# A hybrid two-layer block on one core: values and keys transposed on VectorE and through DRAM, and an output product in another order

## The chip, the cores and the metric

One core of one Trainium2 chip. The metric is the device time of one execution in microseconds (us), the median over runs. The engines named are TensorE (PE), VectorE (DVE), ScalarE (ACT), GpSimd (POOL) and SyncE (SP); each works through its own queue in order, and the chip's 16 DMA engines move data between DRAM and on-chip memory.

## The reference, cut to what matters

The whole program is two layers on 1024 tokens of width 1024, in float32. Layer 0 mixes tokens with retention (four heads) and with a gated delta rule (four heads of 128 by 128), layer 1 with a gated linear recurrence; each is followed by a feed-forward part with a short convolution. The change lies almost wholly in layer 0's delta rule and in the product that ends a mixer:

```python
q_d = l2norm(q_d.reshape(b, t, GDN_HEADS, GDN_DK))
k_d = l2norm(k_d.reshape(b, t, GDN_HEADS, GDN_DK))
...
lmat = jnp.where(strict, jnp.einsum('bhnid,bhnjd->bhnij', k_beta, kc) * decay, 0.0)
rhs = jnp.concatenate([vc * bc, k_beta * jnp.exp(gc)[..., None]], axis=-1)
sol = lax.linalg.triangular_solve(lmat + jnp.eye(c, dtype=jnp.float32), rhs,
                                  left_side=True, lower=True)
...
v_new = u_n - jnp.einsum('bhcd,bhdv->bhcv', w_n, s)
o = jnp.einsum('bhcd,bhdv->bhcv', qd_n, s) + jnp.einsum('bhij,bhjv->bhiv', a_n, v_new)
s = s * cd_n + jnp.einsum('bhcd,bhcv->bhdv', kt_n, v_new)
...
y = jnp.concatenate([y_r, y_d.reshape(b, t, GDN_WIDTH)], axis=-1).astype(hn.dtype)
return y @ w_out
```

The recurrence runs chunk by chunk. The kernel inverts the triangular matrix once per chunk instead of solving with it, and works on eight chunks of 128 tokens.

## The kernel before, in words

Activations lie transposed, channels on the 128 partitions and the 1024 tokens along the free axis, in two halves of 512. Every weight product is made of three matmuls of 128x512 in a reduced format (`mm3`, lines 313 to 315): high part of the weight by high and by low part of the input, low part of the weight by the high part. ACT makes the high part of a weight (L267) and DVE the low part (L268), some steps ahead, from loads that SP issues (L257). This stream of matmuls, "projection" below, fills PE; a counter, `slot`, advances with each group of three, and everything else is hung between the groups: `after(n, f)` runs f n groups later, and a lane (`gdn`, `ret`) is a queue of generators that is taken one step further every so many groups. So the program is written in an order, and a scheduler then sets each engine's queue from it, by which its order can differ from the text's.

The mixer of layer 0, in time: convolutions of keys; A matrices per head; a substitution by rows on 32x32 blocks (`subst`, L1338 its last step on DVE) whose result goes to DRAM (`t_dram`) and comes back by blocks (L1353); then four merges, one per head, that assemble the inverse: 32x32 products L1369, L1378 and L1382, and 64x64 products L1392 and L1398, with ACT's copies L1372, L1385/L1386, L1394 and L1399 between them. The lane's generators for the merges follow `subst`, which yields 11 times after its store. Meanwhile heads of q and v are projected and convolved (`conv_head`, L1264 to L1269), and stored to `q_dram` and `v_dram`.

The scan (`scans`, L1446 on) then goes through the eight chunks. `scan_load` fetches v and q of a chunk. `scan_inside` makes, from a mask (L1453) and exponentials on ACT (L1455, L1457), the scores within the chunk: L1461 transposes v on PE, four heads, and DVE multiplies by a column (L1462); L1465 is keys times q, L1466 its product with the mask; L1473 transposes the keys, and L1474 multiplies them. `scan_state` takes the state through: L1485 keys times state, L1491 the inverse times v, copied by ACT (L1493), L1498 the state's update, L1509 the output, and then `normalise`: squares and sums, a power on POOL (L1422), a multiplication and a transpose on DVE (L1424, L1426), and eight groups later four stores from ACT's queue (L1431). Beside the scan runs retention, with a rotation of its q and k by cosines and sines on DVE (L1538, L1540, L1541) and POOL (L1542).

After the scan the mixer's eight outputs are gated (L1775 for the four of retention), split into high and low parts (ACT L586, DVE L587) and multiplied by the output weights in `part`, four of the inputs at a time (u = 0, 1). For the first half of the tokens the first four outputs form a group with a PSUM bank each: all four take inputs 4, 5, 6, 0 (u = 0), and then each output in turn takes 7, 1, 2, 3 (u = 1). The recurrent mixer of layer 1 ends in the same function.

## Time and profile before

| | |
|---|---|
| median of 3 runs | 2148.48 us (2148.06 to 2148.73) |
| profiled execution, its own time | 2149.09 us |
| its span, first to last instruction | 2147.3 us |
| clock granted to PE | 0.999 |
| PE, DVE, ACT, POOL busy | 99%, 79%, 50%, 5% |
| instructions | 29614 |

The 1.8 us between span and time lie around the span. In the rows of the profile, an engine's group of instructions is given as line, engine, operation, tile written <- tiles read, count, total busy time, mean duration; "idle before" is the time for which the engine stood still ahead of them, and what ended it. Matmuls overlap in the array, so a matmul's duration is longer than the distance from one start to the next.

### The profile page before, as it was taken

How to read it: one execution, taken by the hardware profiler on the slowest of the kernel's cores; microseconds unless marked ns; L12 is line 12 of the kernel's file. 1: busy time of each engine (PE TensorE's matmuls, PEld its weight loads, DVE VectorE, ACT ScalarE, POOL GpSimd, SP SyncE). 2: the span in 40 equal slices, each digit the busy share in tenths (PEclk: the TensorE clock that was granted, in tenths of full speed). 3: DMA queues.
4: the chain of work that ended last, by engine and by line, in shares of the span. 5: the costliest groups of instructions: out<-in, count | busy, mean ns of one | idle time of the engine just before them, and what ended most of it. 6: DMA issues, size and time to landing. Idle time of an engine off the chain costs nothing.

```text
span 2147.3 us, 29614 instructions
## 1 busy us (share of the span) xinstructions
PE 2131.8 (99%) x10652; PEld 1776.5 (83%) x10652; DVE 1704.7 (79%) x2581; ACT 1074.1 (50%) x1732; POOL 96.8 (5%) x114
## 2 busy tenths in 40 slices
PE   9999999999999999999999999999999999999998
PEld 7877888887888888888888888888888888888887
DVE  7995677766999989888766786778999889888645
ACT  6444522234665555555324476755655555554221
POOL 0102022200000000000000000000000000000001
PEclk9999999999999999999999999999999999999999
DMA  5354433543145435438725312252354445375542
GB/s 187 93 168 126 136 94 88 173 146 114 50 163 178 152 141 191 157 113 275 240 99 198 89 50 82 68 157 64 123 181 167 146 154 176 118 267 183 176 169 84
DMA packets 237171, 307.98 MB, mean 143 GB/s; under 512 B 62912, under 2 KB 125920, under 8 KB 237024
## 3 DMA queue, kind: packets, MB, share of 16 engines
q1 hardware_dynamic: 201344, 299.60, 41.8%
q10 hardware_dynamic: 34656, 5.97, 1.5%
q8 instruction: 84, 1.38, 0.3%
q0 software_dynamic: 1024, 0.53, 0.1%
q14 instruction: 63, 0.52, 0.1%
HBM read 215.27 MB, written 90.74 MB: 143 GB/s over the span
## 4 chain that ended last, share of the span: by engine, by line
PE 64%; issue 30%; DVE 3%; DMA 2%; POOL 0%; ACT 0%; SPq 0%; POOLq 0%; DVEq 0%; ACTq 0%
PE ps L313 19%; PE ps L315 19%; PE ps L314 19%; PE pc L313 1%; PE pc L314 1%; PE pc L315 1%; DVE h L973 0%; DVE l L1332 0%; DVE l L1334 0%; PE pc L1491 0%; PE pc L1577 0%; PE pc L1465 0%; PE ps L1509 0%; PE ps L1607 0%; DVE h L1303 0%
## 5 line engine op out<-in xcount | busy, mean ns | idle before, releaser
L313 PE MATMUL ps<-s,whi 128*128 128x512 f32 (+1 forms) x2704 | 1053.6, 390 | 2.5 <-ACT s L586 1.4
L314 PE MATMUL ps<-s,whi 128*128 128x512 f32 (+1 forms) x2704 | 1048.2, 388 | 1.2 <-DVE s L587 0.7
L315 PE MATMUL ps<-s,wlo 128*128 128x512 f32 (+1 forms) x2704 | 1047.5, 388 | 0.0
L267 ACT CAST whi<-raw 128x512 fp32r<-128x512 f32 (+1 forms) x620 | 377.0, 613 | 634.5 <-PE ps L314 499.7
L313 PEld LDWEIGHTS ps<-s,whi 128*128 128x128 f32 x2704 | 507.8, 188 | 108.2 <-ACT s L586 2.3
L314 PEld LDWEIGHTS ps<-s,whi 128*128 128x128 f32 x2704 | 508.0, 188 | 104.5 <-DVE s L900 1.8
L315 PEld LDWEIGHTS ps<-s,wlo 128*128 128x128 f32 x2704 | 507.7, 188 | 104.4 <-DVE wlo L268 0.6
L268 DVE TENSOR_TENSOR wlo<-raw,whi 128x512 fp32r<-128x512 f32 (+1 forms) x620 | 418.0, 680 | 64.0 <-ACT whi L267 55.2
L828 DVE SCALAR_TENSOR_TENSOR t<-halo,cols,t 128x1024 f32<-128x1024 f32 x176 | 221.7, 1281 | 2.1 <-ACT t L826 1.0
L801 DVE TENSOR_TENSOR halo<-ps,kept 128x512 f32<-128x512 f32 (+1 forms) x138 | 92.0, 667 | 76.4 <-PE ps L315 75.6
L811 DVE TENSOR_TENSOR h<-ps,h 128x512 f32<-128x512 f32 x112 | 77.3, 690 | 79.1 <-PE ps L315 79.1
L826 ACT ACTIVATE t<-halo,cols 128x1024 f32<-128x1024 f32 x88 | 109.6, 1247 | 18.0 <-DVE halo L801 9.9
L796 ACT COPY kept<-ps 128x512 f32<-128x512 f32 (+1 forms) x138 | 77.0, 558 | 11.0 <-PE ps L315 9.5
L533 DVE TENSOR_TENSOR h<-ps,h 128x512 f32<-128x512 f32 (+1 forms) x72 | 45.2, 630 | 42.0 <-PE ps L315 41.8
L916 DVE TENSOR_TENSOR t<-t 128x1024 f32<-128x1024 f32 x44 | 53.7, 1221 | 0.0
L911 ACT ACTIVATE t<-t 128x1024 f32<-128x1024 f32 x44 | 46.8, 1063 | 10.0 <-DVE t L828 10.0
L852 ACT CAST t<-t 128x512 fp32r<-128x512 f32 x56 | 34.0, 622 | 34.7 <-DVE t L916 32.7
L401 ACT ACTIVATE t<-h 128x512 f32<-128x512 f32 (+1 forms) x49 | 27.3, 563 | 44.2 <-DVE h L533 44.2
L313 PE MATMUL ps<-s,s 128*128 128x256 f32 (+1 forms) x144 | 46.0, 320 | 0.0
L314 PE MATMUL ps<-s,s 128*128 128x256 f32 (+1 forms) x144 | 45.8, 318 | 0.0
L315 PE MATMUL ps<-s,s 128*128 128x256 f32 (+1 forms) x144 | 45.8, 318 | 0.0
L1266 DVE SCALAR_TENSOR_TENSOR t<-halo,cols,t 128x1024 f32<-128x1024 f32 x33 | 41.9, 1278 | 2.9 <-ACT t L1264 2.6
(337 smaller groups left out, 2113.3 us busy)
## 6 DMA issues: line engine op xcount, KB each, us to landing
raw<-in_ffn_up_dram SPq DMA_DIRECT2D x176, 256.0 KB, 2.7
s<-pf_dram SPq DMA_DIRECT2D x112, 256.0 KB, 5.1
sf_dram<-t SPq DMA_DIRECT2D x72, 256.0 KB, 2.5
raw<-in_ffn_w_dram SPq DMA_DIRECT2D x64, 256.0 KB, 3.0
t<-sf_dram SPq DMA_DIRECT2D x58, 256.0 KB, 4.2
pf_dram<-t SPq DMA_DIRECT2D x56, 256.0 KB, 2.6
pf_dram<-lo SPq DMA_DIRECT2D x56, 256.0 KB, 2.6
raw<-in_mix_in_dram SPq DMA_DIRECT2D x52, 256.0 KB, 3.0
```

What stands on the lines that cost most here:

```text
L267: self.nc.scalar.copy(hi[:, 0:w], raw[:, 0:w])
L268: eng.tensor_tensor(lo[:, 0:w], raw[:, 0:w], f32(hi[:, 0:w]), ALU.subtract)
L313: mm(ps, whi, xhi, start=start, stop=False)
L314: mm(ps, whi, xlo, start=False, stop=False)
L315: mm(ps, wlo, xhi, start=False, stop=stop)
L796: A.copy(kept[o], ps)
L801: V.tensor_tensor(dst(i, j), v(ps), v(kept[k]), ALU.add)
L811: V.tensor_tensor(h(*to[o]), ps.rearrange("p (h c) -> p h c", c=256), h(*to[o]), ALU.add)
L826: A.activation(t, buf[:, 2:2 + T], AF.Identity, scale=w(0), bias=self.col(f"ffn_cb{layer}", tile_i))
L828: V.scalar_tensor_tensor(t, buf[:, 2 + j:2 + j + T], w(j), t, ALU.mult, ALU.add)
L911: A.activation(tg, tg, AF.Silu)
L916: V.tensor_tensor(tg, tg, tv, ALU.mult)
```

## The change

Five things. (1) A convolved head of v is transposed on DVE in 32x32 blocks into the buffer that its convolution no longer needs, and four DMAs from SP's queue store it so that it lies transposed in `v_dram`, in runs of 32 numbers; `scan_load` then brings v as the scan wants it, and L1461's transposes go. (2) Keys are treated likewise: `turn_keys(0)` for heads 0 and 1 after the two gates, `turn_keys(1)` for 2 and 3 after v's first head; their four DMAs each are issued from ACT's queue six groups later, `scan_load` fetches them from a new `k_dram`, and L1473's transposes go. (3) In `normalise` the multiplication and transpose come two groups later, and the stores after nine groups instead of eight. (4) `subst` yields 12 times at its end instead of 11, so that the merges begin later. (5) In `part`, the second four inputs of a group of outputs are taken input by input, each over all the group's outputs, and the sums are added to the residual at the end.

```diff
--- before.py
+++ after.py
@@ -515,6 +515,20 @@
         for ms in groups:
             ps = {m: self.pp(both=True)[:, 0:w] for m in ms}
             for u in range(2):
+                if u == 1 and len(ms) > 1:
+                    hold = self.qpos
+                    ws = [self.quarter((name + "b", m), 0, hold) for m in ms]
+                    for kt in range(len(ys) - 4):
+                        c = slice(kt * P, (kt + 1) * P)
+                        yh, yl = (a[:, c0:c0 + w] for a in ys[4 + kt][n])
+                        for m, (hi, lo) in zip(ms, ws):
+                            self.mm3(ps[m], hi[:, c], lo[:, c], yh, yl, False, kt == len(ys) - 5)
+                            self.slot()
+                    for m in ms:
+                        h = self.H[m][:, sl]
+                        self.nc.vector.tensor_tensor(h, ps[m], h, ALU.add)
+                        each(m, h)
+                    continue
                 for m in ms:
                     if kept is None:
                         hi, lo = self.quarter((name + "ab"[u], m))
@@ -1145,6 +1159,7 @@
         tc = self.tc
         self.q_dram = tc.dram_tile([NCH, P, HALF], F32, name="q_dram")
         self.ry_dram = tc.dram_tile([4, NCH, P, P], F32, name="ry_dram")
+        self.k_dram = tc.dram_tile([NCH, P, HALF], F32, name="k_dram")
         self.v_dram = tc.dram_tile([NCH, P, HALF], F32, name="v_dram")
         self.gc_dram = tc.dram_tile([NH, NCH, P], F32, name="gc_dram")
         self.l_dram = tc.dram_tile([P, 32, 32], F32, name="l_dram")
@@ -1267,7 +1282,10 @@
             th = self.t() if dst is None else dst
             A.activation(th, c, AF.Tanh, scale=0.5)
             V.scalar_tensor_tensor(th, th, 1.0, c, ALU.add, ALU.mult)
+            free[0] = c
             return th
+
+        free = [None]
 
         def conv_head(kind, h, dst):
             unit = conv_unit(kind, h)
@@ -1421,15 +1439,17 @@
                 V.scalar_tensor_tensor(v, v, 1.0 / P, eps, ALU.mult, ALU.add)
             G.tensor_tensor(v, v, self.npow[:, 0:4], ALU.pow)
             on = tmp2(f"on{i}")
-            V.tensor_tensor(ps4(on), ps4(o), bc_last(v, P), ALU.mult)
-
-            V.transpose(s, on)
+
+            def turn():
+                V.tensor_tensor(ps4(on), ps4(o), bc_last(v, P), ALU.mult)
+                V.transpose(s, on)
 
             def post():
                 for a in range(4):
                     bs = slice(32 * a, 32 * a + 32)
                     nc.scalar.dma_start(ydst[:, :, bs], s[bs].rearrange("j (b i) -> j b i", i=32))
-            self.after(8, post)
+            self.after(2, turn)
+            self.after(9, post)
 
         chunk = {}
 
@@ -1445,6 +1465,8 @@
             t.update({"q": tmp2("qc"), "v": spare["v"][n % 2], "e": spare["e"][n % 2], "kt": spare["kt"][n % 2]})
             nc.sync.dma_start(t["v"], self.v_dram[n])
             nc.sync.dma_start(t["q"], self.q_dram[n])
+            if n < NCH - 1:
+                nc.sync.dma_start(t["kt"], self.k_dram[n])
 
         def scan_inside(n):
             cs = slice(n * P, (n + 1) * P)
@@ -1456,10 +1478,7 @@
             for h in range(NH if n else 0):
                 A.activation(gr[:, hs(h)], gr[:, hs(h)], AF.Exp, bias=col(cen, h, n))
             yield
-            pv = self.pc()
-            for h in range(NH):
-                PE.transpose(pv[:, hs(h)], v[:, hs(h)], self.ident)
-            V.tensor_tensor(ps4(v), ps4(pv), bc_last(cn(cv), P), ALU.mult)
+            V.tensor_tensor(ps4(v), ps4(v), bc_last(cn(cv), P), ALU.mult)
             p = self.pc()
             for h in range(NH):
                 PE.matmul(p[:, hs(h)], K[h][:, cs], q[:, hs(h)], start=True, stop=True)
@@ -1468,10 +1487,7 @@
                 V.tensor_tensor(q, q, gr, ALU.mult)
             yield
             if n < NCH - 1:
-                p = self.pc()
-                for h in range(NH):
-                    PE.transpose(p[:, hs(h)], K[h][:, cs], self.ident)
-                V.tensor_tensor(ps4(kt), ps4(p), bc_last(cn(ekt), P), ALU.mult)
+                V.tensor_tensor(ps4(kt), ps4(kt), bc_last(cn(ekt), P), ALU.mult)
             yield
 
         def scan_state(n):
@@ -1696,7 +1712,7 @@
                 subst_step(*sub, j)
                 yield
             subst_store(*sub)
-            yield from range(11)
+            yield from range(12)
         gdn += [subst()]
         for h in range(NH):
             gdn += [together(merge(h, 0), merge(h, 1))]
@@ -1710,16 +1726,36 @@
             if h % 2:
                 values(h // 2)
 
+        def store_turned(dram, x, h, t):
+            V.transpose(t, x)
+            to = dram.rearrange("n (b i) c -> i (n b) c", i=32)
+
+            def store(queue):
+                for d in range(4):
+                    bs = slice(32 * d, 32 * d + 32)
+                    queue.dma_start(to[:, :, h * P + 32 * d:h * P + 32 * d + 32],
+                                    t[bs].rearrange("i (b j) -> i b j", j=32))
+            if dram is self.v_dram:
+                store(nc.sync)
+            else:
+                self.after(6, lambda: store(nc.scalar))
+
+        def turn_keys(i):
+            for h in (2 * i, 2 * i + 1):
+                store_turned(self.k_dram, K[h], h, slots(14 + 2 * (h % 2), 2))
+
         def gates2(heads):
             for h in heads:
                 g = self.gate2(self.unit("mix_in", 12 + h))
                 nc.sync.dma_start(self.g_dram[h], g)
         scan_row(0)
         gates2((0, 1))
+        turn_keys(0)
         for h in range(NH):
             v = conv_head("v", h, None)
-            nc.sync.dma_start(self.v_dram[:, :, hs(h)].rearrange("n p c -> p n c"),
-                              v.rearrange("p (n c) -> p n c", n=NCH))
+            store_turned(self.v_dram, v, h, free[0])
+            if h == 0:
+                turn_keys(1)
         gates2((2,))
         self.flush()
         S = [tmp2("S0"), tmp2("S1")]
```

In the changed file, lines of the scan lie further down: L1453 is L1475, L1455 and L1457 are L1477 and L1479, L1465 is L1484, L1466 L1485, L1491 L1507, L1493 L1509, L1498 L1514, L1509 L1525, L1538, L1540 and L1541 are L1554, L1556 and L1557; in the merge L1369, L1378, L1382, L1392 and L1398 are L1387, L1396, L1400, L1410 and L1416.

**PE, start of the scan.** PE's queue before, from chunk 0's transposes of v (reading tile `kept`) and the products of keys (tiles `h`) and q (tile `l`) on:

```order
L1461 MATMUL pc<-ident,kept 128x128 x4
L1465 MATMUL pc<-l_118,h_88 128x128
L1465 MATMUL pc<-l_118,h_89 128x128
L1465 MATMUL pc<-l_118,h_90 128x128
L1465 MATMUL pc<-l_118,h_91 128x128
L313 MATMUL ps<-s_96,whi 128x512
L314 MATMUL ps<-s_96,whi 128x512
L315 MATMUL ps<-s_96,wlo 128x512
...
L1473 MATMUL pc<-ident,h_88 128x128
L1473 MATMUL pc<-ident,h_89 128x128
L1473 MATMUL pc<-ident,h_90 128x128
L1473 MATMUL pc<-ident,h_91 128x128
```

and now, from the last projection ahead of the same products on:

```order
L315 MATMUL ps<-s_96,wlo 128x512
L1484 MATMUL pc<-l_119,h_88 128x128
L1484 MATMUL pc<-l_119,h_89 128x128
L1484 MATMUL pc<-l_119,h_90 128x128
L1484 MATMUL pc<-l_119,h_91 128x128
L1507 MATMUL pc<-kept,h_92 128x128
L1507 MATMUL pc<-kept,h_93 128x128
...
L1484 MATMUL pc<-l_119,h_88 128x128
...
L1514 MATMUL pc<-kept 128x128 x4
L1525 MATMUL ps<-kept 128x128 x4
L313 MATMUL ps<-s_96,whi 128x512
```

The transposes are gone, and with them the projection that stood between the small products: the products of chunk 0 and the scores of chunk 1 (the second L1484) follow one another directly, behind projection that stood between them before.

**DVE and ACT, start of the scan.** DVE's queue before, from the first rotation (L1538) to the keys' multiplication (L1474):

```order
L1538 TENSOR_TENSOR t<-ps,halo_98 128x512
L1540 TENSOR_TENSOR l_118<-ps,halo_99 64x512
L1541 TENSOR_TENSOR l_118<-ps,halo_99 64x512
L268 TENSOR_TENSOR wlo<-raw,whi 128x512
L1462 TENSOR_TENSOR kept<-pc,l_118 128x512
L1466 TENSOR_TENSOR kept<-kept,pc 128x512
L1474 TENSOR_TENSOR kept<-pc,l_118 128x512
```

and now, from the first to the third rotation and on to the mask of chunk 1 (the second L1475):

```order
L1554 TENSOR_TENSOR t<-ps,halo_98 128x512
L1556 TENSOR_TENSOR l_119<-ps,halo_99 64x512
...
L1554 TENSOR_TENSOR t<-ps,halo_98 128x512
L1556 TENSOR_TENSOR l_119<-ps,halo_99 64x512
L1557 TENSOR_TENSOR l_119<-ps,halo_99 64x512
L1475 TENSOR_TENSOR kept<-kept,l_119 128x512
L1481 TENSOR_TENSOR kept<-kept,l_119 128x512
L1490 TENSOR_TENSOR kept<-kept,l_119 128x512
L1485 TENSOR_TENSOR kept<-kept,pc 128x512
L1475 TENSOR_TENSOR l_119<-l_119 128x512
```

The multiplication of v (L1481) stood after one rotation as L1462, and now stands after three. ACT's queue before, from chunk 0's exponentials to the copy L1493 and on:

```order
L1455 ACTIVATE kept<-kept,l_118 128x128 x2
L1167 ACTIVATE t<-t 128x1024
L1455 ACTIVATE kept<-kept,l_118 128x128 x2
L267 CAST whi<-raw 128x512 x2
L1493 COPY kept<-pc 128x512
L1415 ACTIVATE lo<-ps 128x512
L1455 ACTIVATE kept<-kept,l_118 128x128 x4
L1457 ACTIVATE kept<-kept,l_118 128x128 x4
```

and now:

```order
L1182 ACTIVATE t<-t 128x1024
L1477 ACTIVATE kept<-kept,l_119 128x128 x4
L1477 ACTIVATE l_119<-l_119 128x128 x4
L1479 ACTIVATE l_119<-l_119 128x128 x4
L1509 COPY kept<-pc 128x512
L267 CAST whi<-raw 128x512
L1433 ACTIVATE lo<-ps 128x512
```

The copy (now L1509) stood ahead of chunk 1's eight exponentials, and now stands behind them.

**PE, merges.** Before, the end of the second merge (tile `h_93`) and the start of the third (`h_94`):

```order
L1392 MATMUL pc<-l_118,h_93 64x64 x8
...
L1398 MATMUL pc<-l_118 64x64 x8
L313 MATMUL ps<-s_96,whi 128x512
...
L1369 MATMUL pc<-l_118,h_94 32x32 x16
L313 MATMUL ps<-s_96,whi 128x512
...
L1378 MATMUL pc<-l_118 32x32 x8
L1382 MATMUL pc<-l_118 32x32 x8
L1378 MATMUL pc<-l_118 32x32 x8
```

and now:

```order
L1410 MATMUL pc<-l_119,h_93 64x64 x8
L1416 MATMUL pc<-l_119 64x64 x8
L1387 MATMUL pc<-l_119,h_94 32x32 x16
L313 MATMUL ps<-s_96,whi 128x512
L314 MATMUL ps<-s_96,whi 128x512
L313 MATMUL ps<-s_96,whi 128x512
L314 MATMUL ps<-s_96,whi 128x512
L1396 MATMUL pc<-l_119 32x32
L1400 MATMUL pc<-l_119 32x32
L1396 MATMUL pc<-l_119 32x32 x7
L1400 MATMUL pc<-l_119 32x32 x7
L315 MATMUL ps<-s_96,wlo 128x512
```

Steps that stood twelve matmuls of projection apart follow one another directly or with one to five between; the same goes on to the end of the fourth merge, which comes 37 matmuls after the second one's L1410.

## The prediction

> **What bounds the kernel now.** The page comes first. I read its busy times, and then the clock row and the queues of part 3:
>
> ```profile
> span 2147.3 us, 29614 instructions
> PE 2131.8 (99%) x10652; PEld 1776.5 (83%) x10652; DVE 1704.7 (79%) x2581; ACT 1074.1 (50%) x1732; POOL 96.8 (5%) x114
> PEclk9999999999999999999999999999999999999999
> q10 hardware_dynamic: 34656, 5.97, 1.5%
> ```
>
> TensorE (PE) is busy for all but 15.5 us of the span, at full clock in every slice. A change can win only by taking instructions out of its stream or by closing one of its few waits; it loses whatever it makes PE wait. The waits of PE come next, engine and line, then what it waited for:
>
> ```profile
> PE ps L313 <- ACT s L586: 1.4, 2, 0.9
> PE pc L1369 <- DMA l<-t_dram: 1.0, 2, 0.6
> PE ps L314 <- DVE s L587: 0.7, 1, 0.7
> ```
>
> These waits (total, times, longest) lie in the first merge (L1369) and in the output product (L586, L587). No PE wait belongs to the scan. The profiled execution took 2149.09 us, 0.6 above the median of 2148.48; the sum is made against the former, and 0.6 is taken off at the end. About 0.2% (4.3 us) is what a measurement of this kernel can tell from no change.
>
> **Transposes off PE.** The chain of waits around the start of the scan, start, length, piece:
>
> ```profile
> 263.02 0.44 PE pc L1461 x4
> 263.46 0.89 PE pc L1465 x8
> ...
> 265.75 0.44 PE pc L1473 x4
> ...
> 270.29 0.89 PE pc L1491 x8
> ...
> 275.29 0.89 PE pc L1498 x8
> ```
>
> ```profile
> L1473 PE MATMUL pc<-ident,h 128*128 128x128 f32 x28 | 4.2, 272 | 0.0
> L1424 DVE TENSOR_TENSOR l<-ps,ov 128x512 f32<-128x512 f32 x16 | 11.1, 692 | 14.5 <-POOL ov L1422 13.4 <-PE pc L1491 1.1
> L1426 DVE STREAM_TRANSPOSE lo<-l 128x512 f32<-128x512 f32 x8 | 5.7, 706 | 0.1
> ```
>
> Four transposes hold PE for 0.44 us, though each lasts 272 ns: they are pipelined. Eight sets (L1461) and seven (L1473) go: 15 x 0.44 = -6.6 us. Whoever took the duration for the place in the stream would have 60 x 0.272 = 16.3 us (rival C). The Trainium skill (TensorE: Matmul & The Clock Gate, Part 4: PE-mode transpose) puts a transpose at about 275 ns in one kernel's context; the trace agrees, as a duration.
>
> In their place VectorE (DVE) gets eight transposes of 128x1024, each about two of L1426, so 1.2 to 1.4 us. DVE is idle for a fifth of the span, and neither v nor keys are needed until the scan: 0 on the path, until they delay a conv or a weight split, where each would cost at most its 1.4. The delayed norm multiplication ends DVE's waits for POOL (13.4 us in total at L1424); DVE bounds nothing there: 0.
>
> **The stores.** Before and after, in the view of DMA issues (KB each, us to landing):
>
> ```profile
> v_dram<-t SPq DMA_DIRECT2D x4, 512.0 KB, 4.1
> kept<-v_dram SPq DMA_DIRECT2D x4, 256.0 KB, 3.9
> y_dram<-lo ACTq DMA_DIRECT2D x16, 64.0 KB, 1.9
> ```
>
> ```profile
> 250.79 0.37 SPq L1721 DMA_DIRECT2D v_dram<-t  x1
> 254.51 0.32 SPq L1446 DMA_DIRECT2D kept<-v_dram  x1
> ```
>
> A head is now stored in four DMAs of 1024 runs of 128 B; stores in such runs exist today (y_dram, 512 runs, 1.9 us to landing). The q10 row prices small packets: 1.5% of 16 x 2147.3 us over 34656 is 14.9 ns, so a head takes 4096 x 14.9 / 16 = 3.8 us of all 16 DMA engines, near the 4.1 of today. The last v store goes out at 250.79; some 4 us later (merges and transpose ahead of it) plus 4 x 0.37 to issue and 4.1 to land, v is back from DRAM at about 264 (250.8 + 4 + 1.5 + 4.1 + the load's 3.9), and it is wanted near the row of 275.29: hidden by 10 us, taken at 0. On ScalarE's (ACT's) queue the 16 key stores stand between casts, 16 x 0.37 = 6 us of issuing where ACT is half idle: 0 to 1 on the path, taken 0.
>
> **Merge start and merges.** The merges begin six projection matmuls later, and so the 1.0 us of L1369's waits can go; the turning of v head 0 stands on DVE ahead of the substitution's store and takes some back: -1.0 to 0, taken -0.8. But merges two to four, 60 matmuls apart before, now stand within 37. One merge on PE and on ACT:
>
> ```profile
> 217.12 0.62 PE pc L1369 x32
> ...
> 220.69 0.28 PE pc L1378 x10
> ```
>
> ```profile
> 217.56 1.10 ACT L1372 COPY l<-pc 32x128 f32<-32x128 f32 x4 [2.61 <-PE pc L1369]
> ...
> 221.16 0.55 ACT L1385 ACTIVATE l<-pc 32x128 f32<-32x128 f32 x2 [1.15 <-PE pc L1378]
> ...
> 223.16 0.27 ACT L1386 ACTIVATE l<-pc 32x128 f32<-32x128 f32 x1
> ...
> 225.28 0.37 ACT L1394 COPY l<-pc 64x256 f32<-64x256 f32 x1 [1.21 <-PE pc L1392]
> ```
>
> Each step on PE waits for ACT's copies of the step before: 1.10 us, then 223.16 + 0.27 - 221.16 = 2.27 us, then 0.37, 3.7 in all. Two and a half merges need 9.3 us of such copies, and between them lie 37 x 0.23 = 8.5 us of projection, so most is covered, but not step by step: pairs of steps stand with 0 to 10 matmuls between (at L1410 and L1416 of the changed file, none), and weight casts queue behind copies that wait. I take 2.5 us; the ends are 1 (a copy group bare) and 7 (three quarters of the copies bare).
>
> **The start of the scan.** Here the engines' new order makes a wait that was not there. On PE, L1465, L1491, L1465, L1498 and L1509 stand back to back. On DVE the multiplication of v (changed file's L1481) stands behind three cos/sin groups, the third of which reads the projection that PE ends just before the first L1465. The rows of DVE:
>
> ```profile
> 267.61 0.69 DVE L1538 TENSOR_TENSOR t<-ps,halo 128x512 f32<-128x512 f32 x1 [0.70 <-PE ps L315]
> 268.33 0.69 DVE L1540 TENSOR_TENSOR l<-ps,halo 64x512 f32<-64x512 f32 x1
> 269.06 0.69 DVE L1541 TENSOR_TENSOR l<-ps,halo 64x512 f32<-64x512 f32 x1
> 269.77 0.69 DVE L268 TENSOR_TENSOR wlo<-raw,whi 128x512 fp32r<-128x512 f32 x1
> ```
>
> From that moment, T: the group 2.1 us, the mask L1453 0.6, the multiplication 0.7: v is ready at T + 3.5. PE has 0.89 us of L1465 to do: it waits **2.6 us**. Then ACT:
>
> ```profile
> 255.26 0.70 ACT L1455 ACTIVATE kept<-kept,l 128x128 f32<-128x128 f32 x2
> 256.89 0.68 ACT L1455 ACTIVATE kept<-kept,l 128x128 f32<-128x128 f32 x2
> 271.22 0.59 ACT L1493 COPY kept<-pc 128x512 f32<-128x512 f32 x1 [3.22 <-PE pc L1491]
> L1457 ACT ACTIVATE l<-l 128x128 f32<-128x128 f32 x16 | 5.2, 390 | 0.0
> ```
>
> L1498 needs the copy L1493, and that stands behind L1455 x4 for chunk 0, L1455 x4 and L1457 x4 for chunk 1. The first four run from T + 2.9 to 4.2. The second four need chunk 1's mask, which DVE reaches after the two multiplications and chunk 0's L1466: about T + 5.4. Four L1455 take 1.3 to 1.4, four L1457 1.3, the copy 0.6: T + 8.7. PE, with L1491 and the second L1465 done (0.89 each), is there at T + 5.3: it waits another **3.4 us**. Together 6.0. The lower end is 4 (ACT's second group starting 2 us earlier), the upper 7.2 (each of the 12 operations between them taking 0.1 us more to hand over).
>
> PE's clock row is full everywhere, and the longest of its waits quoted above is 0.9, so this trace does not tell what a wait of 3.4 us does to the clock (rival D). The Trainium skill (TensorE: Matmul & The Clock Gate, Part 1: The HAM clock gate) halves the clock after an idle window of about 3.4 us that is counted freely, until a busy window has passed; no run here shows it, and it would speak against this change.
>
> Later, at two places of the scan, small products stand closer than before: a copy of 0.59 each could show, 0 to 1.2, taken 0.6.
>
> **The output product.** Its waits, on PE and on DVE:
>
> ```profile
> 486.97 0.39 PE L315 MATMUL ps<-s,wlo 128*128 128x512 f32 x1
> 488.26 0.50 PE L313 MATMUL ps<-s,whi 128*128 128x512 f32 x1 [0.90 <-ACT s L586]
> 489.42 0.50 PE L314 MATMUL ps<-s,whi 128*128 128x512 f32 x1 [0.66 <-DVE s L587]
> ...
> 490.90 0.39 PE L314 MATMUL ps<-s,whi 128*128 128x512 f32 x1
> 491.81 0.50 PE L313 MATMUL ps<-s,whi 128*128 128x512 f32 x1 [0.52 <-ACT s L586]
> ```
>
> Start to start 1.29, 1.16 and 0.91 instead of 0.23: 2.7 us lost, because y2 and y3 come late. With the second half run input by input over four outputs, y2 is wanted 18 matmuls (4.1 us) later and y3 22 (5.0 us) later: -2.7. All four weights are now wanted within 12 matmuls; the last one's split may be 0.3 late.
>
> **Sum.** -6.6 - 0.8 - 2.7 + 2.5 + 6.0 + 0.6 = -1.0: 2148.1 against 2149.09, and by the median 2147.5 us. Its own range: the three waits together from 5 (each at its lower end) to 11.7 us (merges 4, scan 7.2, later 0.5) against 10.1 of gains, so 2143.4 to 2150.1; merges beyond 4 are rival B.
>
> **Rivals.**
> (A) The gains come and the waits do not: 2148.48 - 10.1 = 2138.4, or, with the merges' 2.5 left, 2140.9. For it: in the trace of before PE never waits in the scan. Against: DVE and ACT run in order, and v stands behind work that PE itself releases.
> (B) Slower: the merges' copies lie bare. If ACT, where casts and conv activations stand among the copies, becomes the bound between the second merge and the fourth, PE loses 7 us (three quarters of the copies) instead of 2.5; with 7.2 at the scan and 1.2 later the sum is -10.1 + 15.4: 2153.8. It turns slower by over 0.2% when the three waits together pass 14.4 us. Against: ACT is busy for about 11.6 of 20 us there:
>
> ```profile
> 220.00:240.00 20.00, 20.00 (x257) 15.78 (x256) 11.52 (x14) 11.57 (x29) 2.21 (x4) 1.00 0.36 107
> ```
>
> (C) The transposes weigh 16.3 us: 9.7 less, 2137.8. Against it, four within 0.44 us.
> (D) After the scan's wait PE runs at half clock for as long as it waited, 3.4 us: half of that is lost, 2149.2. Nothing in this trace speaks for or against it.
>
> **How the numbers follow.** The forecast has 0.50, A 0.24, B 0.17, C 0.03, D 0.06. The forecast and D lie within 0.2% (2144.2 to 2152.8): 0.56, of which I give 0.04 to faster, where the forecast's range reaches out of it, and 0.02 to slower: same 0.50. Faster: A, C and 0.04: 0.31. Slower: B and 0.02: 0.19. The range leaves out half of A and C below and half of B at most above: 2139.5 to 2153.5.
>
> **What would show it.** In the profile of after: no PE row for the transposes; a PE wait of about 2.6 us for DVE's multiplication of v and one of about 3.4 us for ACT's copy, both at the scan's start near 275 us; PE rows of 0.5 to 1 us waiting for ACT among the merges near 235 us; no wait for L586 in the output product; v loads landed before DVE reaches the multiplication. I am wrong if the scan's start shows less than 4 us of waits in all, or if PE waits for a load of v or keys.

## The result: 0.65% slower, and the profile after

| | before | after |
|---|---|---|
| median of 5 runs | 2148.73 us | 2163.15 us (2158.95 to 2165.64) |
| ratio | 1 | 1.0065, 95% interval 1.0054 to 1.0076 |
| profiled execution, its span | 2149.09, 2147.3 us | 2165.64, 2163.7 us |
| mean granted clock of a run | 0.998 to 0.999 | 0.991 to 0.996 |

The change costs 14.4 us by the medians. The forecast was 2147.5 us and "the same"; the time lies 9.7 us above the upper end of its range.

The page of the changed kernel, the rows that answer to those shown of before:

```profile
span 2163.7 us, 29546 instructions
PE 2140.3 (99%) x10592; PEld 1782.7 (82%) x10592; DVE 1712.8 (79%) x2589; ACT 1070.8 (49%) x1732; POOL 99.7 (5%) x114
PEclk9999899999999999999999999999999999999999
q10 hardware_dynamic: 51296, 8.07, 2.1%
```

PE issues 60 instructions fewer (10592 against 10652), the transposes, and is yet busy for 8.5 us more: the same products take longer. The clock row says where: one slice of it, the fifth, is no longer full. The waits of PE in the changed kernel (total, times, longest) that before did not have:

```profile
PE pc L1507 <- DVE l L1503: 4.8, 3, 3.2
PE pc L1507 <- issue: 3.9, 1, 3.9
PE ps L1622 <- DVE l L1616: 1.7, 1, 1.7
PE pc L1514 <- ACT kept L1509: 0.9, 1, 0.9
```

Together 11.3 us. The output product's wait for L586 is gone. The clock has to be looked at more closely than in slices of 54 us. The view by windows (length, busy time of PE, PEld, DVE, ACT, POOL with counts, then granted clock, DMA share, GB/s):

```profile
236.00:250.00 14.00, 14.00 (x145) 10.48 (x144) 10.94 (x14) 12.17 (x30) 4.39 (x8) 0.50 0.50 97
250.00:260.00 10.00, 10.00 (x117) 7.24 (x117) 4.54 (x6) 7.13 (x17) 0.00 (x0) 0.92 0.24 48
280.00:290.00 10.00, 5.69 (x25) 5.43 (x26) 7.97 (x12) 4.81 (x14) 1.76 (x1) 0.62 0.68 215
290.00:300.00 10.00, 10.00 (x49) 8.65 (x49) 7.73 (x16) 4.19 (x11) 1.04 (x1) 0.87 0.82 240
340.00:360.00 20.00, 16.88 (x101) 14.94 (x101) 14.84 (x28) 5.36 (x13) 4.08 (x3) 0.91 0.35 91
```

From 234.6 to 251.6 us PE does not stand still (its last pause, of 0.26 us, ends at 234.45) and yet runs at half clock: 14.00 us busy in 14 hide it, only the column of the clock shows it. It is at half again from 282.4 to 292.6, and from 343.8 to 347.2 (the ends are from windows of 0.1 us). The three stretches are 17.1, 10.2 and 3.4 us long, 5, 3 and 1 times 3.41 us; what that says is told at the end. Of these 30.7 us PE stands still for some 2; half of the rest, 14 us, is lost.

To set the loss beside the terms of the forecast, I compare the start of the same projection matmul in both traces (the 720th lies behind the merges, the 805th behind the scan's first chunk, the 1090th behind the scan, the 1410th behind the output product), and add back 0.44 us for each set of transposes that had gone by then (4 of 15 up to the 805th). The last two columns are experiments, told below:

| term, us | forecast | after | PE's order held | the same, keys loaded twice |
|---|---|---|---|---|
| transposes | -6.6 | -6.6 | -6.6 | -6.6 |
| merges and their start | +1.7 | +7.5 | +2.0 | +1.9 |
| start of the scan | +6.0 | +9.1 | +2.7 | +2.7 |
| later scan | +0.6 | +9.4 | +12.6 | +5.6 |
| output product | -2.7 | -2.8 | -3.0 | -3.0 |
| sum in the profiled execution | -1.0 | +16.6 | +7.7 | +0.6 |
| median of the runs | | +14.4 | +9.0 | +4.9 |

**The merges.** PE's timeline in the changed kernel (start, length, work, and in brackets the idle time before it and what ended it), where the clock falls:

```profile
231.24 1.14 PE L1410 MATMUL pc<-l,h 64*64 64x64 f32 x16
232.37 1.20 PE L1416 MATMUL pc<-l 64*64 64x64 f32 x16
233.49 0.69 PE L1387 MATMUL pc<-l,h 32*32 32x32 f32 x32
234.45 0.71 PE L313 MATMUL ps<-s,whi 128*128 128x512 f32 x1 [0.26 <-ACT whi L267]
```

Three groups of small products follow each other without a large one, 3.2 us after the last large one a pause of 0.26 us ends, and the next 128x512 takes 0.71 instead of 0.39 us. From here to 251.4 large products start 0.43 us apart instead of 0.23. Among PE's waits between 170 and 262 us stands this pause of 0.26 us alone, and it is for a weight's cast: PE waited for none of ACT's copies there. The loss is the clock's: half of 17.1 us, some 8 of the 8.9 us that the merges cost (7.5 and the 1.4 that their later start gained).

**The scan's start.** DVE, then ACT, then PE in the changed kernel:

```profile
278.61 0.69 DVE L1554 TENSOR_TENSOR t<-ps,halo 128x512 f32<-128x512 f32 x1 [0.55 <-PE ps L315]
279.45 0.69 DVE L1556 TENSOR_TENSOR l<-ps,halo 64x512 f32<-64x512 f32 x1 [0.15 <-POOL t L1558]
280.18 0.69 DVE L1557 TENSOR_TENSOR l<-ps,halo 64x512 f32<-64x512 f32 x1
280.89 0.69 DVE L1475 TENSOR_TENSOR kept<-kept,l 128x512 f32<-128x512 f32 x1
281.50 1.75 DVE L1481 TENSOR_TENSOR kept<-kept,l 128x512 f32<-128x512 f32 x1
...
284.38 0.68 DVE L1475 TENSOR_TENSOR l<-l 128x512 f32<-128x512 f32 x1
```

```profile
285.09 1.28 ACT L1477 ACTIVATE l<-l 128x128 f32<-128x128 f32 x4 [2.19 <-DVE l L1475]
286.28 1.26 ACT L1479 ACTIVATE l<-l 128x128 f32<-128x128 f32 x4
287.44 0.56 ACT L1509 COPY kept<-pc 128x512 f32<-128x512 f32 x1
```

```profile
278.41 1.05 PE L1484 MATMUL pc<-l,h 128*128 128x128 f32 x8
283.36 2.05 PE L1507 MATMUL pc<-kept,h 128*128 128x128 f32 x8 [3.89 <-issue]
285.20 1.91 PE L1484 MATMUL pc<-l,h 128*128 128x128 f32 x8
288.06 2.07 PE L1514 MATMUL pc<-kept 128*128 128x128 f32 x8 [0.95 <-ACT kept L1509]
```

This is the chain that the forecast worked out, link by link. PE's 3.89 us stand under "issue", because the wait's releaser is not recorded; but L1507 starts 0.11 us after DVE's L1481 ends (281.50 + 1.75 = 283.25), and that stands behind the third rotation, which reads the projection that ended at 278.6, and the mask. The second link is there too: mask of chunk 1, ACT's two times four exponentials, the copy, L1514. PE waits only 0.95 us for it because L1507 and L1484 took 1.84 and 1.91 us instead of 0.89 each: the clock had halved 3 us into the first wait.

**The later scan.** DVE before the wait of 3.2 us, and who issued the load (SP):

```profile
337.34 0.69 DVE L1490 TENSOR_TENSOR kept<-kept,l 128x512 f32<-128x512 f32 x1 [2.74 <-DMA kept<-k_dram]
...
339.94 0.69 DVE L1444 TENSOR_TENSOR l<-ps,ov 128x512 f32<-128x512 f32 x1 [0.52 <-POOL ov L1440]
...
341.28 0.70 DVE L1445 STREAM_TRANSPOSE lo<-l 128x512 f32<-128x512 f32 x1
342.00 0.68 DVE L1557 TENSOR_TENSOR l<-ps,halo 64x512 f32<-64x512 f32 x1
342.72 1.12 DVE L1503 SCALAR_TENSOR_TENSOR l<-pc,l 128x128 f32<-128x128 f32 x4
```

```profile
330.46 0.44 SPq L1469 DMA_DIRECT2D kept<-k_dram  x1
```

PE has the product for L1503 ready by 337.2 (L1501 from 336.18) and starts L1507 at 343.12. DVE stands first for 2.74 us at the multiplication of the keys, whose load went out at 330.46, as soon as the state update two chunks before (PE's L1514, 329.38 to 330.43) had read that buffer, and takes 6.8 us to land; then seven operations of rotation and normalisation come ahead of L1503. Over the whole scan, by the view of the line L1490, DVE waits for such loads:

```profile
  DMA kept<-k_dram: 4.1, 2
  DMA l<-k_dram: 3.4, 1
```

Before, the keys came from PE's own transposes, and neither PE nor DVE waited for a DMA in the scan's later chunks.

### The profile page after: what moved, and what is told of

Same layout as the page of the kernel before. It is cut to its first block, busy times and chain, and to the rows that moved or that the text cites. A ratio compares the mean times of both kernels' runs of the same rounds, so it can differ in the third digit from the quotient of the medians.

```text
span 2163.7 us, 29546 instructions
## 1 busy us (share of the span) xinstructions
PE 2140.3 (99%) x10592; PEld 1782.7 (82%) x10592; DVE 1712.8 (79%) x2589; ACT 1070.8 (49%) x1732; POOL 99.7 (5%) x114
## 4 chain that ended last, share of the span: by engine, by line
PE 65%; issue 29%; DVE 2%; DMA 2%; POOL 1%; ACT 0%; SPq 0%; POOLq 0%; DVEq 0%; ACTq 0%
PE ps L313 19%; PE ps L315 19%; PE ps L314 19%; DMA kept<-k_dram 1%; PE pc L313 1%; PE pc L314 1%; PE pc L315 1%; PE ps L1573 0%; PE ps L1575 0%; DMA raw<-in_mix_in_dram 0%; PE ps L1574 0%; DVE h L987 0%; PE pc L1514 0%; PE pc L1507 0%; PE pc L1593 0%
## 5 line engine op out<-in xcount | busy, mean ns | idle before, releaser
L268 DVE TENSOR_TENSOR wlo<-raw,whi 128x512 fp32r<-128x512 f32 (+1 forms) x620 | 416.0, 677 | 46.1 <-ACT whi L267 38.9
L842 DVE SCALAR_TENSOR_TENSOR t<-halo,cols,t 128x1024 f32<-128x1024 f32 x176 | 221.4, 1280 | 2.1 <-ACT t L840 1.0
L547 DVE TENSOR_TENSOR h<-ps,h 128x512 f32<-128x512 f32 (+1 forms) x64 | 39.6, 621 | 34.4 <-PE ps L315 34.2
L373 DVE TENSOR_TENSOR halo<-ps,R 128x512 f32<-128x512 f32 x36 | 24.6, 686 | 32.4 <-PE ps L315 32.3
```

The source lines that it names most:

```text
L268: eng.tensor_tensor(lo[:, 0:w], raw[:, 0:w], f32(hi[:, 0:w]), ALU.subtract)
L842: V.scalar_tensor_tensor(t, buf[:, 2 + j:2 + j + T], w(j), t, ALU.mult, ALU.add)
```

## The experiments

In each, "the change" is the whole change; ratios are to the kernel before, with 95% intervals. My theory (theory 1 below) was that the loss comes from PE's new order: the merges crowd together, the scan's first products stand back to back, and each brings waits and half clock. Its rivals: the stores and VectorE's added work cost the time in any order; and (theory 3) VectorE's queue in the later scan does, where the state's update stands behind the keys' multiplication. What else an expectation calls a theory it states itself.

### Which parts cost

**The output product alone** (before, plus part 5).

```diff
+                if u == 1 and len(ms) > 1:
...
+                    continue
```

> The kernel before with nothing changed but the output product's order. The order of the engines ahead of it stays that of before, so there is no half clock and no new wait. Both theories: the three gaps of 2.7 us close, 2146.0 us.

2145.97 us (2145.07 to 2148.71), ratio 0.9991 (0.9982 to 1.0000); the 1410th matmul comes 2.9 us earlier against the 1090th. As forecast.

**Without the keys** (part 2 undone).

```diff
-        turn_keys(0)
...
-                turn_keys(1)
```

> The changed kernel with the keys transposed on TensorE again (their seven sets of transposes back, 3.1 us). Its queues differ: the merges are still bunched, in two clumps instead of one, and the scan's first products still stand back to back. Theory 1 (the queue order bunches small products, the array's clock halves there and PE waits): half clock at both places, 2155 to 2163. Theory 2 (the stores in runs of 128 bytes make loads and copies late): half of those stores are gone and with them about half of the loss, 2153 to 2156, and no half clock without a wait of PE ahead of it.

2147.61 us, ratio 1.0001 (0.9992 to 1.0010): neither expectation. The keys are worth 14 to 15 us of loss (by the ratios and by the medians). Values alone still halve the clock (257.4 to 264.2) and lose 4.2 us over merges and scan's start, but only 2.1 in the later scan. At the scan's start PE waits 0.5 us, for ACT's copy; the wait for the multiplication of v is not there.

**Without the values** (part 1 undone).

```diff
-            store_turned(self.v_dram, v, h, free[0])
+            nc.sync.dma_start(self.v_dram[:, :, hs(h)].rearrange("n p c -> p n c"),
+                              v.rearrange("p (n c) -> p n c", n=NCH))
```

> The changed kernel with the values transposed on TensorE again (eight sets back, 3.5 us). Its merges are bunched as in the changed kernel, but the scan's first products stand apart again. Theory 1: half clock in the merges alone, some 9 us lost there, nothing at the scan: -2.7 -3.1 -0.8 +9 = +2.4, 2151 (2148 to 2155). Theory 2: half of the stores, half of the loss: 2153 to 2156, with late loads.

2152.53 us, ratio 1.0019 (1.0010 to 1.0029), as theory 1 had it. The keys alone bring the crowded merges (7.0 us by the 720th matmul, half clock from 242 to 252) and nothing at the scan's start, so that the wait of 3.9 us there takes values and keys together; 3.9 us are lost in the later scan.

**Without the two groups' delay** (part 3 undone).

```diff
+            V.tensor_tensor(ps4(on), ps4(o), bc_last(v, P), ALU.mult)
+
+            V.transpose(s, on)
...
-            self.after(2, turn)
-            self.after(9, post)
+            self.after(8, post)
```

> The changed kernel with the normalisation's multiplication, transpose and stores at their old places (after zero and eight groups). Merges and scan start are bunched as before. If the delayed normalisation is what puts VectorE's work ahead of the state's update, the later chunks lose less and the time falls by 2 to 5 us, 2158 to 2161; if it helps, as it is meant to, the time rises or stays, 2163 to 2167.

2161.05 us (2155.93 to 2163.41), ratio 1.0054 (1.0040 to 1.0067): inside the scatter of the whole change.

**Neither values nor keys** (before, plus parts 3, 4 and 5).

```diff
+            self.after(2, turn)
+            self.after(9, post)
...
-            yield from range(11)
+            yield from range(12)
```

> The changed kernel without the turning of values and keys: the output product's order, the delayed normalisation and the later merges alone. The engines' order keeps its even spacing. Both theories: clock full, the gaps of the output product and the wait at the first merge gone, 2148.4 - 2.7 - 0.7 = 2145.0 (2144 to 2146.5).

2146.05 us, ratio 0.9986 (0.9977 to 0.9994), full clock throughout. With the output product alone the best version of all, below the time before; parts 3 and 4 cost and bring nothing that shows.

### What lowers the clock

The next five add products whose results are not used or are the same again; their own time is counted.

**64x64 products four times over**, in every merge, on top of the output product alone.

```diff
+            for _ in range(4):
+                for c in range(4):
+                    PE.matmul(q[:, c, :], l4[64:128, c, 0:64], w1[64:128, c, 64:128], start=True, stop=True)
```

> The kernel with the output product's new order alone (2146 us, clock full), and in each merge the 64x64 products of one step issued four times over into the same place: about 0.7 us of small products per issue, eight issues of which become thirty-two, 4 x 1.3 us or more in a row without a wait between them. It puts nothing new in the queues of the other engines. Theory 1a (the clock's gate counts a stretch of small products as idle, though TensorE never stops): half clock after some of the merges, with no pause ahead of it, and more time lost than the added products' 16 us: above 2165. Theory 1b (only a pause lowers the clock): clock full, 2146 + 16 = 2162.

One run: 2156.51 us at a clock of 0.999; stretches of 3.87 us of these products leave the clock alone.

**Sixteen times over**, in one merge.

```diff
+            for _ in range(16 if h == 1 else 1):
```

> As the run with products issued four times over, but sixteen times and in the second merge alone: two stretches of about 15 us with nothing but 64x64 products on TensorE and no wait between them. Any window of 3.4 us, however placed, lies wholly inside. Theory 1a (small products alone count as idle): half clock from some 3 to 7 us into the stretch, its second part twice as slow, and the whole above 2185. Theory 1b (only pauses count): clock full, 2146 + 30 x 0.97 = 2175.

One run: 2159.81 us, clock 0.999. PE's timeline and a window of it:

```profile
205.63 15.14 PE L1407 MATMUL pc<-l,h 64*64 64x64 f32 x256
```

```profile
210.00:215.00 5.00, 5.00 (x89) 5.00 (x88) 0.00 (x0) 1.50 (x3) 0.00 (x0) 1.00 0.00 0
```

15 us of nothing but 64x64 products keep full clock: products of that size by themselves are not the cause.

**32x32 products sixteen times over**, in one merge.

```diff
+            for _ in range(16 if h == 1 else 1):
+                for c in range(4):
+                    for o in (0, 64):
+                        lo, up = slice(o, o + 32), slice(o + 32, o + 64)
+                        PE.matmul(q[lo, c, :], l4[up, c, lo], w0[up, c, up], start=True, stop=True)
```

> The output product's change alone (2146.0 us, full clock), with the second merge's 32x32 products of L1369 issued sixteen times over, added work that changes no result. Theory 1c, the 32x32 products of the bunched merges are what lowers the granted clock: a stretch of some 10 us of nothing but them is followed by half clock, mean clock 0.996 or less, and the time is 2146 plus the products' own time plus 3 us or more. Theory 1d, small products do not lower it, pauses do: mean clock 0.998 or more, and the time is 2146 plus the products' own time (about 10 us) within 1.5 us.

One run: 2163.54 us, clock 0.995. PE's timeline, and a window:

```profile
198.86 2.90 PE L1384 MATMUL pc<-l,h 32*32 32x32 f32 x171
203.82 7.33 PE L1384 MATMUL pc<-l,h 32*32 32x32 f32 x255 [2.06 <-issue]
212.08 2.51 PE L1384 MATMUL pc<-l,h 32*32 32x32 f32 x86 [0.93 <-issue]
214.51 0.80 PE L313 MATMUL ps<-s,whi 128*128 128x512 f32 x1
```

```profile
205.00:210.00 5.00, 4.86 (x182) 4.72 (x180) 0.79 (x1) 0.51 (x2) 0.00 (x0) 0.50 0.40 114
```

At full clock one takes 2.90 / 171 = 17 ns, so the 480 added ones are worth 8.1 us; the rest of 17.5 us is pauses and clock. PE is 97% busy in that window at half clock, and 7 us of 32x32 products do not bring the clock back, which some 3 us of large ones then do. This is the opposite of the 64x64 products, and what theory 1c expected. The first fall, though, follows a pause of 2.06 us in the issue, so the run does not show that 32x32 products alone would have started it.

**Large products among the merges** (48 unused 128x512 matmuls, 48 x 0.229 = 11.0 us, two ahead of most steps).

```diff
+        def fill(n):
...
+                PE.matmul(p, x[:, 0:P], x, start=True, stop=True)
...
-            q = q4(self.pc())
+            q = q4(fill(2 if h else 0))
```

> The changed kernel with two more 128x512 matmuls, whose result nothing reads, ahead of each small step of merges two to four: 48 of them, 11 us of work. The bunched order stays. Theory 1 (the array's clock is halved because the stretch holds hardly any large matmuls): the clock stays full there, which gives back about 8 us, and pauses are filled: 2163 + 11 - 8 - 2 = 2164 (2160 to 2168), mean clock 0.995 or more. Rival (the loss there is the copies' waiting, the clock follows from something else): half clock stays, 2170 to 2175.

2170.72 us, ratio 1.0105 (1.0090 to 1.0120): the time is in the rival's band, the clock is as theory 1 had it. It stays full through the merges, in the same crowded order:

```profile
240.00:250.00 10.00, 10.00 (x139) 6.75 (x134) 8.65 (x12) 9.42 (x22) 3.94 (x8) 1.00 0.58 122
```

Of 11.0 us of added work 4.5 come back: the merges proper, which lost 8.9 us in the change, here lose 4.4 besides the fill. Those 4.4 are not waits, for PE stands still nowhere between 170 and 270 us of this run. They are the price of alternating. From the last large product to the first small one it is 0.33 us from start to start, from the first large one after small ones to the next 0.34, both instead of 0.23, and some 0.1 more from the last small one to the large; and from the 400th to the 720th matmul small products now stand in 30 places between large ones, before the change in 16. So the run takes away the clock's loss and puts a loss of its own there. What bare copies would cost it does not show.

**Large products in the scan's first wait** (16 ahead of the first L1507).

```diff
+            for _ in range(0 if n else 16):
+                PE.matmul(p, x[:, 0:P], x, start=True, stop=True)
```

> The changed kernel with sixteen more 128x512 matmuls, whose result nothing reads, between the scan's first two small products, where TensorE waits about 4 us for VectorE: 3.6 us of work in place of a pause. Theory 1: no half clock there, 10 us of which lost about 4: 2159 (2157 to 2161). Rival (the clock there is lowered by the small products, not by the pause): half clock stays, 2163 or a little above.

2165.59 us, ratio 1.0083 (1.0066 to 1.0099). The first wait was filled and the clock held through it, but now a weight's cast, which waited for its load, stood ahead of the copy in ACT's queue, PE waited 5.1 us for the copy, and the clock halved there. The time is on the rival's side, but the run moved the wait, and tells nothing of the cause.

### The order of PE's queue

**Held in the written order from the projection of q to the end of the scan.**

```diff
+        with self.tc.manual_schedule(engines={mybir.EngineType.PE}):
+            for h in range(NH):
+                q = conv_head("q", h, None)
```

> The changed kernel, all its operations and stores kept, with TensorE's queue held to the order in which the program is written, from the q heads to the end of the scan: merges twelve matmuls apart and the scan's small products six or more apart, as before the change. Theory 1: the clock stays full and the waits go; the gains of 10.1 us are left: 2139 (2137 to 2142). Theory 2: the stores are all there, so the loss is too: above 2155, with PE waiting for loads of v or keys.

2172.06 us, ratio 1.0115 (1.0102 to 1.0129): missed. It lost its time ahead of the merges already, where the written order puts small products too early:

```profile
PE pc L1257 <- DVE l L1254: 5.2, 1, 5.2
PE pc L1309 <- DVE h L1321: 4.5, 1, 4.5
```

So it tells nothing of the merges.

**Held in the scan only**, the merges as in the change.

```diff
+        with self.tc.manual_schedule(engines={mybir.EngineType.PE}):
+            gdn += [scans()]
...
+            for h in range(NH):
+                q = rot_head(h)
```

> The whole change with PE's queue held in the written order from the scan's first step to the gates' last head, so that the merges stay bunched and the keys' and values' stores stay, and only the scan's queue is as before. Theory (order): the merges still lose their 9 us, the scan's start loses under 3 us instead of 8, the clock is full there; 2155 to 2160 us. Rival (the stores, the loads and VectorE's work, whatever PE's order): the scan's start keeps its waits and its half clock, 2161 us or more.

2165.31 us, ratio 1.0081 (1.0065 to 1.0096): on the rival's side. By the 720th matmul 6.6 us are lost, as in the change; at the scan's start PE came to a load of q that was still under way:

```profile
PE pc L1484 <- DMA l<-q_dram: 6.3, 1, 6.3
```

That load goes out at 272.8 us, in the change at 273.5, behind the last store of v in both; the held order only has its reader earlier. So the run does not part the order from the loads.

**Held from just before the merges to the end of the scan.**

```diff
+        with self.tc.manual_schedule(engines={mybir.EngineType.PE}):
+            scan_row(0)
+            gates2((0, 1))
+            turn_keys(0)
...
+            for h in range(NH):
+                q = rot_head(h)
```

> The whole change with PE's queue held in the written order from before the merges to the end of the scan, the part ahead of it scheduled freely, all stores kept. Theory (order): merges lie evenly, 12 groups of projections apart, the clock stays full through them and through the scan's start; the 9 us of the merges go, and most of the 8 us of the scan's start; what is left is the later scan's wait of the state update on VectorE, up to 9.7 us, against 10 us of transposes and output product gained: 2143 to 2153 us, clock 0.997 or more. Rival (the stores and the added work on VectorE bring the loss in any order): 2158 us or more.

2157.08 us (2153.19 to 2159.99), ratio 1.0042 (1.0030 to 1.0055): 5 to 6 us better than the change (by the ratios and by the medians), with every store and load kept, and between the two expectations. Its windows over the merges and the scan's start:

```profile
240.00:250.00 10.00, 8.71 (x109) 6.49 (x108) 4.08 (x5) 6.55 (x18) 0.00 (x0) 1.00 0.38 67
280.00:290.00 10.00, 9.42 (x52) 7.89 (x51) 7.60 (x16) 4.19 (x12) 2.33 (x2) 1.00 0.52 152
```

Merges 12 projection matmuls apart and a scan whose first products have projections between them: full clock, 2.0 us lost in the one place and 2.7 in the other, against 7.5 and 9.1. So the new order of PE's queue, not the stores or VectorE's transposes as such, made those two losses. Two things qualify this. With PE's queue other things moved as well: the last store of v goes out at 255.6 us instead of 268.3, and chunk 0's load of v at 262.0 instead of 274.1. And PE still waits 2.5 us at the scan's start, without half clock, and 2.9 us for ACT's copies in the merges, which are bare here. What remains is the later scan:

```profile
PE pc L1507 <- DVE l L1503: 6.1, 3, 3.3
```

### The later scan

**The keys' multiplication on POOL** (the change otherwise).

```diff
-                V.tensor_tensor(ps4(kt), ps4(kt), bc_last(cn(ekt), P), ALU.mult)
+                G.tensor_tensor(ps4(kt), ps4(kt), bc_last(cn(ekt), P), ALU.mult)
```

> The changed kernel with the keys' multiplication on GpSimd instead of VectorE. Theory 3 (in the later chunks VectorE, which works in order, stands at that multiplication and waits for the keys' load, with the state's update and so TensorE behind it; about 5 of the 9.7 us lost there): those waits of L1507 for L1503 go from 4.8 us to under 2, and the time falls by 3 to 7 us, to 2156 to 2160. Theory 2 (the stores alone): no change, 2163.

2169.54 us, ratio 1.0100 (1.0085 to 1.0115): slower. The load's wait went to POOL's queue, and PE's wait for retention's step (L1622) grew from 1.7 to 3.6 us.

**Keys loaded for two chunks only** (the change otherwise; from the third chunk the loads are left out and old keys are multiplied).

```diff
-            if n < NCH - 1:
+            if n < 2:
                 nc.sync.dma_start(t["kt"], self.k_dram[n])
```

> The changed kernel with the keys' load left out from the third chunk on, so that the later multiplications take what lies in their two buffers. All multiplications, transposes and stores stay. Theory 3 (the later chunks' loss comes from waiting for the keys' loads on VectorE): of the 9.7 us lost between the scan's second chunk and its end 4 or more go, 2156 to 2160. Rival (VectorE's order there, with the normalisation and rotation ahead of the state's update, costs the same without the load): 2162 to 2165.

2162.89 us (2158.21 to 2164.60), ratio 1.0061 (1.0045 to 1.0076). The median lies in the rival's band. In the profile the later scan loses 4.4 us instead of 9.4, but the output product gains 0.8 instead of 2.8, and the runs spread over 6 us by their clock: from the medians this run decides nothing.

**The same with PE's order held.**

```diff
+        with self.tc.manual_schedule(engines={mybir.EngineType.PE}):
+            scan_row(0)
...
-            if n < NCH - 1:
+            if n < 2:
                 nc.sync.dma_start(t["kt"], self.k_dram[n])
```

> PE's order held through merges and scan as in the run before (2157.1 us), and the keys loaded for the first two chunks only, so that later chunks multiply the keys that lie in the buffer already; the output differs for it. Everything else, VectorE's order too, as there. Theory 4 (in the later scan the state update stands in VectorE's queue behind the keys' multiplication, which waits 2.3 to 2.8 us for its load): two such waits go, and the half clock behind them (3.4 us): 2149 to 2152 us, clock 0.998 or more. Rival 4b (VectorE has that much work ahead of the state update anyway, and the load's wait only hides it): within 2 us of 2157.

2152.74 us (2150.50 to 2154.72), ratio 1.0021 (1.0012 to 1.0030): 4.3 us under the run with the loads (1.0021 against 1.0042; the intervals meet at 1.0030), and 0.7 above the expected band. In the profile the later scan falls from 12.6 to 5.6 us, and PE's waits for the state's products from 6.1 to

```profile
PE pc L1507 <- DVE l L1503: 0.6, 2, 0.3
```

The loads of keys are the larger part of the later scan's loss. A pause of 1.9 us for ACT at L1608 now brings half clock of its own, for 3.4 us.

**VectorE's order held as well**, and the keys' multiplication written at the head of the state's step.

```diff
+        with self.tc.manual_schedule(engines={mybir.EngineType.PE, mybir.EngineType.DVE}):
+            scan_row(0)
...
             s0, s1 = S[n % 2], S[(n + 1) % 2]
+            if n < NCH - 1:
+                V.tensor_tensor(ps4(kt), ps4(kt), bc_last(cn(ekt), P), ALU.mult)
```

> The whole change, PE's and VectorE's queues both held in the written order through merges and scan, and the keys' multiplication written right ahead of the state update that it belongs to, one step later than in the change, so that it finds its load landed. Theory 4: no wait for a load of keys on VectorE, the state update stands behind ready work only; 2143 to 2151 us, clock 0.998 or more. Rival 4b: the written order of VectorE has waits of its own (the normalisation's power on POOL), and the later scan still loses its 8 us: 2155 us or more.

2160.60 us, ratio 1.0058 (1.0045 to 1.0072): missed. DVE no longer waits for a load of keys; but the written order loses 11 us before the 720th matmul,

```profile
PE pc L1416 <- ACT l L1412: 8.3, 2, 5.6
PE pc L1507 <- DVE l L1503: 5.2, 3, 2.6
```

and in the later scan L1503 still stands behind normalisation (with its own wait for POOL) and rotation: 8.9 us lost there. The time is rival 4b's, and its wait for POOL is seen.

**Without the keys, PE's order held.**

```diff
+        with self.tc.manual_schedule(engines={mybir.EngineType.PE}):
+            scan_row(0)
...
-        turn_keys(0)
```

> PE's order held through merges and scan, the change without its keys (they are transposed on PE again, nothing of them is stored or loaded). Theory (the rest of the loss is the keys' alone: their load, and the multiplication in VectorE's queue): 2143 to 2148 us, below the time before by 1 us or more. Rival (values and the normalisation's two groups cost the later scan as well): 2150 us or more.

2155.21 us, ratio 1.0040 (1.0026 to 1.0053): the rival's side, but for a reason of neither: the first merge met its load,

```profile
PE pc L1386 <- DMA l<-t_dram: 5.2, 1, 5.2
```

and half clock after it; 7.4 us are lost by the 720th matmul, nothing at the scan's start, 5.0 in the later scan. A held order is right only for the program that it was held in.

## Why the prediction was wrong, point by point

**Right.** The transposes' price (60 instructions off PE; rival C is out) and the output product (-2.7 forecast; -2.8 in the profile, and 2145.97 for it alone). The merges' start: -0.8 forecast, -1.4 measured. The scan's start in mechanism: both waits are there, at the lines named, 4.8 us together. v was back from DRAM in time, though by less than the 10 us forecast: the load went out at 274.12 us, landed at 277.5, and DVE took it up at 281.50. Neither sign of being wrong came: the scan's start shows more than 4 us of waits, and PE itself waits for no load of v or keys; DVE does.

**Failed: "I take 2.5 us" for ACT's copies in the merges.** The merges lost 8.9, but not so. The rows "of 0.5 to 1 us waiting for ACT among the merges" are missing: PE's one pause there is 0.26 us, for a cast. What cost the time is the clock, 17.1 us at half, brought on by the small products standing together; at half clock the projection between the steps also takes longer (0.43 us from start to start instead of 0.23), and so covers more of the copies. What the copies cost at full clock in this order no run shows. Where the merges lie evenly (PE's order held), PE waits 2.9 us for them, and merges and start together cost 2.0, against the 1.7 forecast for both: near, but in another order.

**Mis-sized: 6.0 us for the scan's start.** 9.1. The first wait was 3.9 instead of 2.6, mostly since one multiplication on DVE took 1.75 instead of 0.69 us (a price that the trace of before shows at other operations; see the end). The half clock then stretched the next products by some 4.1 us (half of 10.2 less the 2.0 of standing still), and the second wait shrank to 0.95 behind them.

**Failed: "Later, at two places of the scan, small products stand closer than before ... taken 0.6".** 9.4. That step looked at PE's order alone. What counts there is who feeds PE: the keys' multiplication on DVE now waits for a load which can start only when a buffer two chunks old is free, and needs 7 us; the state's update stands behind it in the same queue. Without those loads 5.6 remain, without the keys altogether 5.0 (both with PE's order held), so that about 7 of 12.6 are the loads'. Of the 5.6, the pause at L1608 and half of the 3.4 us at half clock behind it are 3.6. In the free order the loss is 2.1 without the keys and 3.9 without the values, so 9.4 takes both. Normalisation and rotation ahead of L1503 are seen in the trace, but no run took them away alone.

**Failed: rival D, a chance of 0.06 and 1.7 us.** It was given one place, the scan's wait, and half of that wait. The clock was low for 30.7 us in three places, some 14 us lost, and the largest had no wait to speak of: only small products in a row. The Trainium skill (TensorE: Matmul & The Clock Gate, Part 1: The HAM clock gate) lowers the clock after an idle window of about 3.4 us; the runs agree with the length (3.41 us), but in the merges PE was busy, with 64x64 and 32x32 products and one pause of 0.26 us. The recovery agrees as well: the clock came back at 251.6, after 3.4 us of nothing but large products from 248.2 on.

**Rival B** named the direction and the merges, with 2153.8, but its cause, bare copies, is not in the trace. The three places together passed its point of decision, 14.4 us, with 26.0, of which some 14 are the clock.

Open: what each size of product counts for the clock, for which only an estimate from the traces stands below, and what the rest of the later scan's loss is made of.

## What to carry to other kernels

A change that takes instructions out of a full engine also takes away what stood between its other instructions: look at which small products become neighbours, and price a stretch of about 3 us without large ones at half of the time until some 3 us of large ones have run. Where a computed operand becomes a loaded one, work out when its buffer comes free and when the load lands, and then walk the in-order queue of its first reader for whoever stands behind. Before a multi-part change is kept or dropped, time its parts: here one part won 2.4 us and two others hid it.

## What the hardware showed that was not expected

- Full use of PE at half clock: 14 us with PE 100% busy and the clock at 0.50, in the merges; 15.14 us of 64x64 products alone at full clock; 7 us of 32x32 products that stay at half.
- The clock moves in steps of 3.41 us. In the runs that have any, each stretch of half clock ahead of the program's end is 1 to 5 times 3.41 us long, and the stretches of one run lie whole clock steps apart (read from the clock's column in windows of 0.1 us and less): in the changed kernel they begin at 234.58, 282.36 and 343.80 us, 14 and 18 clock steps apart.
- This decides which pauses are followed by half clock. Of PE's pauses between 1.9 and 3.1 us some were, each lying in one clock step: 1.93 us (PE's order held, keys loaded twice), 2.27 us (PE's order held), 2.72 us (PE's order as written). Some were not: 3.10 us, which the end of a clock step cuts into 1.75 and 1.34 (large products among the merges), and 2.55 us, cut into 0.69 and 1.86 (PE's order held). That the scan's start kept full clock in the last of these runs is in part luck of where the clock step ended.
- It also decides the merges. The clock step ahead of the fall, 231.2 to 234.6 us, holds 2.26 us of 64x64 products, 0.69 of 32x32, 0.26 of standing still and 0.20 of large ones; without the values, one with 1.58, 0.69, 0.26 and 0.87 us was not followed by half clock. An estimate from all traces, some 12 000 clock steps: with 64x64 products counted at half and 32x32 ones at nothing, PE's work comes to 1.59 us or less in all 32 clock steps ahead of a fall, and to 1.53 or more in all others but one (1.40). No run tests these weights alone.
- One multiplication of 128x512 on DVE (L1481) took 1.75 us instead of 0.68, while a POOL product beside it took 1.76 instead of 1.28 (280.94 to 282.70). Before, as L1462, it read PE's result in `pc`, now it reads `kept`, which a load fills. That goes with the price: of the two-operand DVE operations of 128x512 that began during a POOL product of that size, in the traces of before and after, the 20 that read one of PE's tiles (`pc`, `ps`) took 0.67 to 0.69 us (L1462 at 264.32: 0.68), and the 17 that read none 0.68 to 1.80, all but one over 0.80 (L268 at 415.82, before: 1.79).
- Stores in runs of 128 B landed in 3.8 (v) and 4.3 us (keys) for 128 KB; the loads of 256 KB at the scan's start took between 3.2 and 7.4 us, where before those of v took 2.6 and 2.8.
